# S5 scan states: from a transpose on VectorE and TensorE to a ScalarE copy and two DMAs through DRAM

## The chip, the cores and the metric

The kernel runs on one core of one Trainium2 chip. Times are device microseconds of one execution, from the core's own clock. The kernel before took 1846.21 us, the median of 3 runs (1843.55 to 1846.67).

A core has five engines, each with a queue of its own that it works through strictly in order: TensorE (PE: matmuls; its weight loads are shown as PEld), VectorE (DVE), ScalarE (ACT), GpSimd (POOL) and SyncE (SP, which here only issues DMAs). DMAs can be issued from the queues of SP, ACT and POOL. The profile shows 16 DMA engines behind them.

## What is computed

A trunk of two layers on 256 frames of width 2048, in float32: a gated linear attention layer, then an S5 layer (a complex-diagonal state-space model), each with adaLN modulation and a post-LayerNorm residual. Everything that matters here is in the S5 mixer:

```
proj = u_in @ w_in
u, z = jnp.split(proj, 2, axis=-1)
...
_, _, x_r, x_i = lax.associative_scan(_linear_recurrence_combine, (a_r, a_i, bu_r, bu_i), axis=1)
return jnp.einsum('blgp,gip->blgi', x_r, cr_b) - jnp.einsum('blgp,gip->blgi', x_i, ci_b)
...
y = jax.nn.gelu(y)
y = y * jax.nn.sigmoid(y @ w_glu + b_glu)
y = y * jax.nn.silu(z)
return y @ w_out
```

The 4096 channels are 256 groups of 16; each group has 64 complex states.

## The kernel before

**Chunks.** The recurrence isn't run frame by frame. The 256 frames are 32 chunks of 8. For every chunk the kernel computes the sum of the inputs that reach the chunk's end, runs the recurrence over the 32 chunk states (`scan`, L1180), and then forms the outputs of a chunk as two matmul products: the eight inputs of the chunk by an in-chunk kernel (`mt`), and the state at the chunk's start by powers of the transition times C (`wc`). The groups are worked in 32 blocks, numbered f, of eight groups each. The states of all blocks lie in one buffer, `sx`, with the state index on the partitions and chunk, real/imaginary and group in the free dimension; its first half holds f 0 to 15, its second half f 16 to 31.

**The projections.** `st_step` (L171) does a step of a projection: 24 matmuls of 128x256. Each weight tile is split into a rounded part (`hi`, a cast on ScalarE, L145) and a remainder (`lo`, a subtraction on VectorE, L146), because one product is made of three. There are four buffers for weight tiles and three each for the two parts, so a cast waits until TensorE has finished the step three before. The u projection (`su`) runs first, with the inputs of the chunks beside it; then the z projection (`sz`), 64 steps in eight groups (loop at L1270).

**The output side** runs beside `sz`. A list `bg` holds small pieces of work; after each projection step `pump` (L96) takes `Y_RATE` pieces from it on average. For each f the list has, in this order: three scan steps of the second half (while there are any), `cside(f)`, `xstage(f - 1)`, `ystage(f - 2)`: 126 pieces over 56 steps.

- `cside(f)` (L1263) loads the next block of C rows and powers (`cload`, three DMAs into `cl`, since the third third of the columns is the first one with the real and imaginary halves of the partitions swapped), loads the in-chunk kernel `mt` (`mload`, 512 KB), and multiplies `cl` to the two weights `wc` on VectorE (L1074, L1075).
- `xstage(f)` (L1236) makes the chunk states an operand of TensorE: a 32x32-block transpose on VectorE from `sx` to `xT`, two 128x128 transposes on TensorE into PSUM (`psxs`), and a copy on ScalarE to `xS`.
- `ystage(f)` (L1247) does 48 small matmuls (`psy`), a transpose on VectorE (`yt`) and a GELU on ScalarE into `U`.

The C rows, B rows and powers come from `rec` in DRAM. They are written there from GpSimd's queue much earlier, during the first layer (`prep_b`, `prep_c`, `prep_pow`).

**What sets the order.** The program is written in the order of these calls, and the order on each engine is then made by a scheduler, which moves an instruction ahead when it expects its operands to be ready. So an instruction of `bg` may stand several projection steps away from where the list puts it. Semaphore waits follow from the buffers: an instruction that writes a tile waits until the last reader of that buffer is done, and a DMA counts as a reader until it has landed.

Of the kernel before, what the change touches and what calls it, by code (L numbers as in the profile page):

```python
# [8 lines left out]
F32 = mybir.dt.float32  # L9
# [6 lines left out]
P = 128  # L16
D = 2048
E = 4096
T = 256
# [14 lines left out]
def trunk(ctx, tc, x, c, ln_g, ln_b, ada_w, ada_b, gla_w_in, gla_gate_w2, gla_gate_b, gla_norm_g,  # L34
# [45 lines left out]
    def psx(name):  # L80
        return ax.tile([P, 512], F32, tag="ax", name=name)
# [10 lines left out]
    bg = []  # L92
# [506 lines left out]
    def prep_pow(t):  # L599

        pw = SM["pw"]
        pd = s8t(f"pd{t}", [8, 2, 2, 64])
        for h in range(2):
            S.copy(pd[:, :, :, h, :], pw[:, :, :, t * 64:t * 64 + 64])
        lc = s8t(f"lc{t}", [16, 2, 8, 8])
        for ri in range(2):
            for nb in range(2):
                ps = psx(f"pspw{t}{ri}{nb}")
                for i in range(4):
                    n = nb * 4 + i  # L610
# [3 lines left out]
        wdma(rec[:, 16 * t:16 * t + 16, 128:256], lc.rearrange("p f r g n -> p f (r g n)"))  # L614

    def to_rows(src, i_of, t, o, nm):
        got = {}

        def step(ib):
            if ib == 0:  # L620
                got["a"] = s8t("rows" + nm, [128, 16])
            a = got["a"]
            ps = psx(f"psr{nm}{ib}")
            for i in range(4):
                PE.transpose(ps[:, i * P:(i + 1) * P], i_of(src(), 4 * ib + i), ident)
            S.copy(a[:, :, 4 * ib:4 * ib + 4].rearrange("p g i -> p i g"), ps.rearrange("p (i g) -> p i g", i=4))
            if ib == 3:
                av = a.rearrange("p (f g) i -> p f (g i)", f=16)
                wdma(rec[:, 16 * t:16 * t + 16, o:o + 128], av)

        return [lambda ib=ib: step(ib) for ib in range(4)]

    def prep_b(t):
        got = {}

        def load():
            bi = s8t(f"bin{t}", [2, 64, 16])
            got["bi"] = bi
# [17 lines left out]
        return [load], [comp] + to_rows(lambda: got["b"], lambda s, i: s[:, :, i], t, 256, f"b{t}")  # L656

    def prep_c(t):
        got = {}

        def load():
            ci = s8t(f"cin{t}", [2, 16, 64])
            got["ci"] = ci
            dma(ci[:, 0], s5_c_re[0, t * P:(t + 1) * P])
            dma(ci[:, 1], s5_c_im[0, t * P:(t + 1) * P])

        def comp():
            ci = got["ci"]
# [5 lines left out]
        return [load], [comp] + to_rows(lambda: got["c"], lambda s, i: s[:, i].rearrange("g r p -> g (r p)"), t, 0, f"c{t}")  # L674
# [376 lines left out]
    def bload(f2):  # L1051

        a = tp.tile([P, 2, 384], F32, tag="rb", name=f"rb{f2}", bufs=2)
        dma(a[:, :, 0:256], rec[:, 2 * f2:2 * f2 + 2, 128:384])
        for h in range(2):
            dma(a[64 * h:64 * h + 64, :, 256:384], rec[64 - 64 * h:128 - 64 * h, 2 * f2:2 * f2 + 2, 256:384])
        rb[f2] = a

    rc = {}
# [1 line left out]
    def kload(f2):  # L1061

        a = rc[f2] = tp.tile([P, 2, 144], F32, tag="rc", name=f"rc{f2}", bufs=2)
        dma(a, rec[:, 2 * f2:2 * f2 + 2, 0:144])

    wb = {}

# [144 lines left out]

    def cload(f):
        a = tp.tile([P, 384], F32, tag="cl", name=f"cl{f}", bufs=2)
        dma(a[:, 0:256], rec[:, f, 0:256])
        for h in range(2):
            dma(a[64 * h:64 * h + 64, 256:384], rec[64 - 64 * h:128 - 64 * h, f, 0:128])
        cl[f] = a

    def cunit(f):  # L1220
        a = cl[f]
        w = [tp.tile([P, 8, 8, 16], F32, tag=f"wc{i}", name=f"wc{i}{f}", bufs=2) for i in range(2)]
        powmul(w[0], w[1], a[:, 0:128], a[:, 256:384], a[:, 128:256])
        wc[f] = w

    kap = dk[:, :]
# [6 lines left out]

    xss = {}

    def xstage(f):  # L1236
        xt_ = tp.tile([P, 2, 4, 32], F32, tag="xt", name=f"xT{f}", bufs=1)
        n = 2 * (f % 16)
        V.transpose(xt_, sx[:, f // 16, 0:32, :, n:n + 2].rearrange("p c r b -> p b r c"))
        px = psx(f"psxs{f}")  # L1240
        for b in range(2):
            PE.transpose(px[:, b * P:(b + 1) * P], xt_[:, b].rearrange("p r l -> p (r l)"), ident)
        xs = tp.tile([P, 2, 128], F32, tag="xs", name=f"xS{f}", bufs=2)
        S.copy(xs, px[:, :T].rearrange("p (b r) -> p b r", b=2))
        xss[f] = xs

    def ystage(f):  # L1247
        xs = xss[f]
        py = psx(f"psy{f}")
        U = Uv(f)  # L1250
        for b in range(2):
            o = py[:, b * P:(b + 1) * P]
            for q in range(4):
                PE.matmul(o[32 * q:32 * q + 32], lhsT=U[:, 2 * q + b], rhs=mt[f][:, :, 2 * q + b, :], start=True, stop=False)
# [6 lines left out]
        S.activation(U, yt, AF.Gelu_apprx_tanh)  # L1261

    def cside(f):  # L1263
        if f < 31:
# [5 lines left out]
    for g in range(8):  # L1270
        banks = [psm(f"sz{g}{f}") for f in range(4)]
        for kp in range(8):
            w = split(wload(sw, 2 * kp, E + g * 512, f"sz{g}{kp}"), f"sz{g}{kp}")
            st_step(banks, u1, w, kp, 15)
            if g == 0:
                bstep(1 + kp % 2)
            pump(SCAN_RATE if g == 0 else Y_RATE)
        for f in range(4):
            i = (g * 4 + f) % 8
            if g % 2 == 0 and f == 0:  # L1280
                zs.append(s8t(f"zs{g // 2}", [8, T]))
# [172 lines left out]
```

## Time and profile before

| | us |
|---|---|
| median of 3 runs | 1846.21 |
| the profiled execution | 1847.81 |
| its span, first to last instruction | 1846.0 |
| ScalarE busy over the span | 895.7 |
| GpSimd busy over the span | 85.6 |
| one state transpose on VectorE (median of 32) | 0.633 |
| one `wc` product on VectorE (median of 32) | 1.218 |
| `mt`, issue to landing (median of 32) | 7.7 |

The profile is of one execution. "Busy" counts an engine's instructions, but matmuls are pipelined and their durations overlap, so the cost of a matmul is read from the distance between two starts. A row of the timeline gives start, duration, engine, line, operation, output and inputs; in brackets is how long the engine stood idle before it, and what released it. The DMA share of a window is the mean busy share of the 16 DMA engines.

### The profile page before, as it was taken

The page shows a single profiled execution, that of the slowest core. Times are in us where ns is not written, and L with a number is a line of the kernel's source. Part 1 is how long each engine was busy: PE and PEld are TensorE (multiplying, and loading weights), DVE is VectorE, ACT ScalarE, POOL GpSimd, SP SyncE. Part 2 cuts the span into 40 slices and gives each one's busy share as a digit, 9 for nine tenths or more (in the row PEclk, how much of TensorE's full clock was granted, in tenths as well). Part 3 has the DMA queues.
Part 4 walks back from the last instruction along what each step waited for, and adds up shares of the span by engine and source line. Part 5 has one row for each costly group of instructions (what it writes and reads, how often), then busy time and mean ns, then how long its engine had stood idle before and what let it go on. Part 6 is the DMA issues. An engine that isn't in the chain of part 4 may idle for free.

```text
span 1846.0 us, 33780 instructions
## 1 busy us (share of the span) xinstructions
PE 1795.7 (97%) x13555; PEld 1587.8 (86%) x13555; DVE 1401.8 (76%) x1862; ACT 895.7 (49%) x1266; POOL 85.6 (5%) x94
## 2 busy tenths in 40 slices
PE   7999999999999999999999999999999999999997
PEld 5776897899999888799998989989888888888885
DVE  4877667879989988686799779888677775557556
ACT  4432557555556333554454444545544544444332
POOL 0000000000000000002232300000000000000000
PEclk9999999999999999999999999999999999999998
DMA  9996885889889998577666567899788886668653
GB/s 342 380 325 226 293 263 165 262 270 322 290 277 324 331 356 287 171 248 212 197 175 196 173 194 219 232 254 240 220 276 267 270 277 209 190 192 325 193 183 92
DMA packets 246101, 457.86 MB, mean 248 GB/s; under 512 B 19828, under 2 KB 49198, under 8 KB 244662
## 3 DMA queue, kind: packets, MB, share of 16 engines
q1 hardware_dynamic: 239320, 436.02, 73.8%
q0 software_dynamic: 5856, 18.63, 3.1%
q8 instruction: 106, 1.74, 0.4%
q10 hardware_dynamic: 768, 1.05, 0.2%
q14 instruction: 51, 0.42, 0.1%
HBM read 437.01 MB, written 18.61 MB: 247 GB/s over the span
## 4 chain that ended last, share of the span: by engine, by line
PE 83%; DVE 9%; DMA 3%; issue 2%; ACT 2%; POOL 0%; SPq 0%; DVEq 0%; ACTq 0%; POOLq 0%
PE gl L192 13%; PE gl L193 7%; PE op L168 6%; PE op L167 6%; PE op L169 6%; PE z L182 3%; PE z L180 3%; PE z L181 3%; PE v L168 3%; PE v L169 3%; PE v L167 3%; PE su L180 2%; PE su L181 2%; PE su L182 2%; PE sz L180 2%
## 5 line engine op out<-in xcount | busy, mean ns | idle before, releaser
L146 DVE TENSOR_TENSOR logl<-wgl,higl 128x1024 fp32r<-128x1024 f32 x128 | 156.6, 1223 | 115.7 <-ACT higl L145 109.2
L145 ACT CAST higl<-wgl 128x1024 fp32r<-128x1024 f32 x128 | 134.4, 1050 | 170.7 <-PE gl L192 163.0
L192 PE MATMUL gl<-yp,higl 128*128 128x512 f32 x512 | 179.3, 395 | 0.1
L192 PE MATMUL gl<-yb,higl 128*128 128x512 f32 x512 | 179.1, 395 | 0.0
L145 ACT CAST hio<-wo 128x1024 fp32r<-128x1024 f32 x95 | 100.2, 1055 | 154.7 <-PE op L169 134.4
L146 DVE TENSOR_TENSOR loo<-wo,hio 128x1024 fp32r<-128x1024 f32 x95 | 116.1, 1223 | 67.1 <-ACT hio L145 66.6
L315 DVE SCALAR_TENSOR_TENSOR acc<-wa,cs,acc 128x512 f32<-128x512 f32 x217 | 162.1, 747 | 4.0 <-DMA wa<-in_ada_w 1.1
L180 PE MATMUL sz<-u1h,hisz 128*128 128x256 f32 x512 | 151.0, 295 | 1.3 <-ACT zs L1282 1.2
L180 PE MATMUL su<-u1h,hisu 128*128 128x256 f32 x512 | 151.8, 298 | 0.0
L180 PE MATMUL z<-u0h,hiz 128*128 128x256 f32 x512 | 148.7, 290 | 0.0
L182 PE MATMUL sz<-u1h,losz 128*128 128x256 f32 x512 | 145.6, 285 | 3.1 <-DVE losz L146 3.1
L182 PE MATMUL su<-u1h,losu 128*128 128x256 f32 x512 | 146.7, 287 | 0.0
L181 PE MATMUL su<-u1l,hisu 128*128 128x256 f32 x512 | 146.4, 286 | 0.0
L182 PE MATMUL z<-u0h,loz 128*128 128x256 f32 x512 | 144.9, 283 | 0.6 <-DVE loz L146 0.6
L181 PE MATMUL sz<-u1l,hisz 128*128 128x256 f32 x512 | 145.4, 284 | 0.0
L181 PE MATMUL z<-u0l,hiz 128*128 128x256 f32 x512 | 144.7, 283 | 0.0
L193 PE MATMUL gl<-yb,logl 128*128 128x256 f32 x512 | 142.9, 279 | 0.0
L193 PE MATMUL gl<-yp,logl 128*128 128x256 f32 x512 | 142.2, 279 | 0.0
L145 ACT CAST hisz<-wsz 128x1024 fp32r<-128x1024 f32 x64 | 67.0, 1050 | 117.7 <-PE sz L181 62.0
L192 PEld LDWEIGHTS gl<-yp,higl 128*128 128x128 f32 x512 | 95.9, 188 | 22.8 <-issue 0.7
L192 PEld LDWEIGHTS gl<-yb,higl 128*128 128x128 f32 x512 | 96.0, 188 | 22.6
L168 PE MATMUL v<-lov,u0h 128*128 128x512 f32 x256 | 103.6, 406 | 6.9 <-DVE lov L146 6.8
(321 smaller groups left out, 4974.0 us busy)
## 6 DMA issues: line engine op xcount, KB each, us to landing
wgl<-in_s_w_glu SPq DMA_DIRECT2D x128, 512.0 KB, 4.5
wa<-in_ada_w SPq DMA_DIRECT2D x116, 512.0 KB, 5.3
wv<-in_gla_w_in SPq DMA_DIRECT2D x64, 512.0 KB, 5.8
wz<-in_gla_w_in SPq DMA_DIRECT2D x64, 512.0 KB, 5.1
wsu<-in_s_w_in SPq DMA_DIRECT2D x64, 512.0 KB, 4.3
wsz<-in_s_w_in SPq DMA_DIRECT2D x64, 512.0 KB, 5.7
wo<-in_s_w_out SPq DMA_DIRECT2D x64, 512.0 KB, 4.6
a<-in_ada_w SPq DMA_DIRECT2D x31, 1024.0 KB, 10.8
```

What stands on the lines that cost most here:

```text
L145: S.copy(hi, w)
L146: last_lo[0] = V.tensor_tensor(lo, w, hi.bitcast(F32), op=ALU.subtract).ins
L167: PE.matmul(banks[tt], lhsT=uh, rhs=hi[:, kk, :], start=(k == first), stop=False)
L168: PE.matmul(banks[tt], lhsT=uh, rhs=lo[:, kk, :], start=False, stop=False)
L169: last_mm[0] = PE.matmul(banks[tt], lhsT=ul, rhs=hi[:, kk, :], start=False, stop=(k == last)).ins
L180: PE.matmul(o, lhsT=wh, rhs=u.hi(k), start=(k == first), stop=False)
L181: PE.matmul(o, lhsT=wh, rhs=u.lo(k), start=False, stop=False)
L182: last_mm[0] = PE.matmul(o, lhsT=wl, rhs=u.hi(k), start=False, stop=(k == last)).ins
L192: PE.matmul(banks[f], lhsT=hi[:, kk, fs], rhs=u.both(k), start=(k == 0), stop=False)
L193: PE.matmul(banks[f][:, :T], lhsT=lo[:, kk, fs], rhs=u.hi(k), start=False, stop=(k == last))
L315: V.scalar_tensor_tensor(acc[0], w[:, kk, :], cs[:, k:k + 1], acc[0], op0=ALU.mult, op1=ALU.add)
```

## The change

The state of block f no longer goes through a VectorE transpose and two TensorE transposes. ScalarE copies it from `sx` to `xT` in another order of the free dimension (`xwrite`) and writes it to a DRAM tile `dx[f]` with a DMA from its own queue (128 KB, 1 KB for each partition). A DMA from GpSimd's queue (`xread`) reads it back with the partition index made of chunk and real/imaginary, in runs of 256 bytes, into `xS`. `xT` has one buffer, as before; `xS` has three instead of two, `yt` one instead of two.

Since the partitions of `xS` now come in another order (chunk before real/imaginary), the weights `wc` must have that order too: `cload` permutes the rows as it reads `rec`, and the swapped third is stored in `rec` (which grows from 384 to 512 columns), so that `cload` is one DMA instead of three. That takes two more GpSimd writes after each of the two C row tiles. The other edits in `rec` move columns only. The list `bg` has 158 pieces now, with `xwrite` one block ahead of `xread`, and `Y_RATE` is 2.9.

```diff
-    rec = dp.tile([P, 32, 384], F32, name="rec")
+    rec = dp.tile([P, 32, 512], F32, name="rec")
+    dx = dp.tile([32, P, 256], F32, name="dx")
...
                 wdma(rec[:, 16 * t:16 * t + 16, o:o + 128], av)
+                if o == 128:
+                    for h in range(2):
+                        wdma(rec[64 * h:64 * h + 64, 16 * t:16 * t + 16, 0:128], av[64 - 64 * h:128 - 64 * h])
...
-    Y_RATE = 2.311
+    Y_RATE = 2.9
...
     def cload(f):
         a = tp.tile([P, 384], F32, tag="cl", name=f"cl{f}", bufs=2)
-        dma(a[:, 0:256], rec[:, f, 0:256])
-        for h in range(2):
-            dma(a[64 * h:64 * h + 64, 256:384], rec[64 - 64 * h:128 - 64 * h, f, 0:128])
+        dma(a, rec[:, f, 0:384].rearrange("(r l) x -> l r x", r=4))
...
-    def xstage(f):
-        xt_ = tp.tile([P, 2, 4, 32], F32, tag="xt", name=f"xT{f}", bufs=1)
+    def xwrite(f):
+        xt_ = tp.tile([P, 4, 2, 32], F32, tag="xt", name=f"xT{f}", bufs=1)
         n = 2 * (f % 16)
-        V.transpose(xt_, sx[:, f // 16, 0:32, :, n:n + 2].rearrange("p c r b -> p b r c"))
-        px = psx(f"psxs{f}")
-        for b in range(2):
-            PE.transpose(px[:, b * P:(b + 1) * P], xt_[:, b].rearrange("p r l -> p (r l)"), ident)
-        xs = tp.tile([P, 2, 128], F32, tag="xs", name=f"xS{f}", bufs=2)
-        S.copy(xs, px[:, :T].rearrange("p (b r) -> p b r", b=2))
-        xss[f] = xs
+        S.copy(xt_, sx[:, f // 16, 0:32, :, n:n + 2].rearrange("p c r b -> p r b c"))
+        S.dma_start(dx[f], xt_.rearrange("p r b c -> p (r b c)"))
+
+    def xread(f):
+        xs = xss[f] = tp.tile([P, 4, 2, 32], F32, tag="xs", name=f"xS{f}", bufs=3)
+        wdma(xs.rearrange("p q b c -> p q (b c)"), dx[f].rearrange("(q l) (r x) -> (l r) q x", q=4, r=4))
...
-                    PE.matmul(o[32 * q:32 * q + 32], lhsT=xs[:, b, 32 * q:32 * q + 32],
+                    PE.matmul(o[32 * q:32 * q + 32], lhsT=xs[:, q, b],
...
-        yt = tp.tile([P, 8, 32], F32, tag="yt", name=f"yt{f}", bufs=2)
+        yt = tp.tile([P, 8, 32], F32, tag="yt", name=f"yt{f}", bufs=1)
...
-                if 1 <= f < 33:
-                    bg.append(lambda f=f: xstage(f - 1))
+                for i in range(0 if f == 0 else f + 1, min(f + 2, 32)):
+                    bg.append(lambda i=i: xwrite(i))
+                if f < 32:
+                    bg.append(lambda f=f: xread(f))
```

Three places show what the scheduler makes of it. In the names, the number behind `hisz`, `wsz` and `sz` is the group of the z projection and the step in it, the number behind `xT`, `xS`, `psxs` and `psy` is f.

ScalarE's queue in the middle of the stage, around the step 4, 6. Before:

```order
L145 CAST hisz45_12955<-wsz45_12953 128x1024
L1261 ACTIVATE U1_7510<-yt8_12760 128x8x32
L1244 COPY xS10_12808<-psxs10_12805 128x256
L145 CAST hisz46_13030<-wsz46_13028 128x1024
L1261 ACTIVATE U1_7510<-yt9_12835 128x8x32
L1244 COPY xS11_12883<-psxs11_12880 128x256
```

After:

```order
L145 CAST hisz45_12947<-wsz45_12945 128x1024
L1241 COPY xT19_13336<-sx_7511 128x256
L1242 DMA dx_200<-xT19_13336 128x256
L1241 COPY xT20_13407<-sx_7511 128x256
L1242 DMA dx_200<-xT20_13407 128x256
L145 CAST hisz46_12988<-wsz46_12986 128x1024
L1262 ACTIVATE U1_7515<-yt9_12800 128x8x32
L1241 COPY xT21_13478<-sx_7511 128x256
L1242 DMA dx_200<-xT21_13478 128x256
```

The copies of the states no longer keep pace with f: they stand well ahead of the GELU of their own block, up to two of them between two casts. In the whole queue the copies xT0 to xT15 stand behind the 12th to the 25th cast of the z projection and xT16 to xT31 behind the 35th to the 46th, the second half after the last scan step.

TensorE's queue, at the end of a projection step that is followed by psy. Before:

```order
L182 MATMUL sz53_13148<-u1h0_7385,losz52_13295 128x256
L1242 MATMUL psxs16_13324<-ident_89,xT16_13322 128x128 x2
L1254 MATMUL psy15_13329<-mt15_13127,U1_7510 32x128 x4
L1257 MATMUL psy15_13329<-wc015_13129,xS15_13222 32x128 x4
L1257 MATMUL psy15_13329<-wc115_13130,xS15_13222 32x128 x4
```

After:

```order
L181 MATMUL sz53_13125<-u1l0_7392,hisz52_13240 128x256
L182 MATMUL sz53_13125<-u1h0_7390,losz52_13241 128x256
L1255 MATMUL psy15_13270<-mt15_13048,U1_7515 32x128 x4
L1258 MATMUL psy15_13270<-wc015_13050,xS15_13087 32x128 x4
L1258 MATMUL psy15_13270<-wc115_13051,xS15_13087 32x128 x4
```

The two transposes are gone; psy follows the projection directly and stands behind the same projection step as before.

SP's queue where the output side begins. Before:

```order
L136 DMA wsz16_11666<-in_s5_w_in 128x2x512
L1215 DMA cl0_11398<-rec_197 128x256
L1217 DMA cl0_11398<-rec_197 64x128 x2
L1215 DMA cl1_11478<-rec_197 128x256
L1217 DMA cl1_11478<-rec_197 64x128 x2
L1231 DMA mt0_11482<-dk_198 128x1x1024
L1231 DMA mt1_11564<-dk_198 128x1x1024
```

After:

```order
L136 DMA wsz16_11665<-in_s5_w_in 128x2x512
L1219 DMA cl0_11403<-rec_197 128x1x384
L1219 DMA cl1_11481<-rec_197 128x1x384
L1233 DMA mt0_11483<-dk_198 128x1x1024
L1233 DMA mt1_11571<-dk_198 128x1x1024
L136 DMA wsz17_11729<-in_s5_w_in 128x2x512
```

Each cl is one DMA, and the next weight tile stands two blocks of cl earlier than before.

More of the change, by code (lines that the diff above doesn't have):

```diff
@@ L613, in prep_pow @@
                 S.activation(lc[:, :, ri, :, nb * 4:nb * 4 + 4].rearrange("p f g n -> p n f g"), pv, AF.Identity, scale=sgn if ri else 1.0)
-        wdma(rec[:, 16 * t:16 * t + 16, 128:256], lc.rearrange("p f r g n -> p f (r g n)"))
+        wdma(rec[:, 16 * t:16 * t + 16, 256:384], lc.rearrange("p f r g n -> p f (r g n)"))
     def to_rows(src, i_of, t, o, nm):
@@ L654, in comp @@
             got["b"] = bb.rearrange("g r p i -> g (r p) i")
-        return [load], [comp] + to_rows(lambda: got["b"], lambda s, i: s[:, :, i], t, 256, f"b{t}")
+        return [load], [comp] + to_rows(lambda: got["b"], lambda s, i: s[:, :, i], t, 384, f"b{t}")
     def prep_c(t):
@@ L672, in comp @@
             got["c"] = cc
-        return [load], [comp] + to_rows(lambda: got["c"], lambda s, i: s[:, i].rearrange("g r p -> g (r p)"), t, 0, f"c{t}")
+        return [load], [comp] + to_rows(lambda: got["c"], lambda s, i: s[:, i].rearrange("g r p -> g (r p)"), t, 128, f"c{t}")
     (lb0, cb0), (lc0, cc0), (lb1, cb1), (lc1, cc1) = prep_b(0), prep_c(0), prep_b(1), prep_c(1)
@@ L1053, in bload @@
         a = tp.tile([P, 2, 384], F32, tag="rb", name=f"rb{f2}", bufs=2)
-        dma(a[:, :, 0:256], rec[:, 2 * f2:2 * f2 + 2, 128:384])
+        dma(a[:, :, 0:256], rec[:, 2 * f2:2 * f2 + 2, 256:512])
         for h in range(2):
-            dma(a[64 * h:64 * h + 64, :, 256:384], rec[64 - 64 * h:128 - 64 * h, 2 * f2:2 * f2 + 2, 256:384])
+            dma(a[64 * h:64 * h + 64, :, 256:384], rec[64 - 64 * h:128 - 64 * h, 2 * f2:2 * f2 + 2, 384:512])
         rb[f2] = a
@@ L1063, in kload @@
         a = rc[f2] = tp.tile([P, 2, 144], F32, tag="rc", name=f"rc{f2}", bufs=2)
-        dma(a, rec[:, 2 * f2:2 * f2 + 2, 0:144])
+        dma(a, rec[:, 2 * f2:2 * f2 + 2, 128:272])
     wb = {}
@@ L1222, in cunit @@
         w = [tp.tile([P, 8, 8, 16], F32, tag=f"wc{i}", name=f"wc{i}{f}", bufs=2) for i in range(2)]
-        powmul(w[0], w[1], a[:, 0:128], a[:, 256:384], a[:, 128:256])
+        powmul(w[0], w[1], a[:, 128:256], a[:, 0:128], a[:, 256:384])
         wc[f] = w
@@ L1256, in ystage @@
                 for q in range(4):
-                    PE.matmul(o[32 * q:32 * q + 32], lhsT=xs[:, b, 32 * q:32 * q + 32],
+                    PE.matmul(o[32 * q:32 * q + 32], lhsT=xs[:, q, b],
                               rhs=w[:, 2 * q + b].rearrange("p n i -> p (n i)"), start=False, stop=(w is wc[f][-1]))
-        yt = tp.tile([P, 8, 32], F32, tag="yt", name=f"yt{f}", bufs=2)
+        yt = tp.tile([P, 8, 32], F32, tag="yt", name=f"yt{f}", bufs=1)
         V.transpose(yt, py[:, :T].rearrange("p (b t i) -> p t b i", b=2, t=8))
-        S.activation(U, yt, AF.Gelu_apprx_tanh)
+        S.activation(U, yt.rearrange("p t c -> p (t c)").rearrange("p (b r) -> p b r", b=2), AF.Gelu_apprx_tanh)
     def cside(f):
```

## The prediction

> **What bounds the kernel now.** I read the page's busy times first, then a table of windows over the stage that the change touches, then the instructions behind single tiles, and last the order of the new program.
>
> ```profile
> PE 1795.7 (97%) x13555; PEld 1587.8 (86%) x13555; DVE 1401.8 (76%) x1862; ACT 895.7 (49%) x1266; POOL 85.6 (5%) x94
> ```
>
> TensorE is busy nearly throughout, so only what shortens TensorE's stream, or what makes it wait, can move the end. The table of windows cuts the z projection of the S5 layer from 1085 us on, where the output side of the scan runs in the background.
>
> ```profile
> 1085.00:1164.00 79.00, 78.70 (x926) 75.33 (x925) 76.31 (x139) 36.02 (x53) 0.00 (x0) 0.99 0.79 229
> 1164.00:1212.00 48.00, 48.00 (x714) 44.98 (x714) 43.37 (x49) 24.53 (x38) 0.00 (x0) 1.00 0.90 242
> 1212.00:1254.00 42.00, 40.11 (x563) 37.61 (x565) 33.42 (x39) 21.28 (x32) 0.00 (x0) 0.96 0.99 247
> 1254.00:1294.00 40.00, 40.00 (x608) 37.18 (x602) 37.78 (x46) 24.61 (x43) 0.00 (x0) 1.00 0.98 246
> ```
>
> The columns are PE, PEld, DVE, ACT and POOL busy, then clock, DMA share and GB/s. To 1164 VectorE (76.31 of 79) and TensorE are both full, because the scans of the second half run there; afterwards TensorE is full, and the DMA engines go from 0.90 to 0.99 busy. ScalarE is about half busy everywhere. So three resources stand close together here, and a change that relieves two of them meets the third.
>
> **What goes.** The tile view of the transposed states, the same tile's instructions alone in the first window (PE, PEld, DVE), and the longest wait of TensorE at the stage's start:
>
> ```profile
> L1242 PE MATMUL psxs<-ident,xT x64: 270/272/328, 1079.9 to 1288.5; 128*128 128x128 f32 x64
> L1239 DVE STREAM_TRANSPOSE xT<-sx x32: 572/633/665, 1073.9 to 1284.5; 128x256 f32<-128x256 f32 x32
> L1244 ACT COPY xS<-psxs x32: 351/354/394, 1080.9 to 1289.9; 128x256 f32<-128x256 f32 x32
> ...
> 1085.00:1164.00 79.00, 3.37 (x18) 2.20 (x18) 5.78 (x9) 0.99 0.79 229
> PE sz L182 <- DVE losz L146: 3.1, 1, 3.1
> ```
>
> Matmuls overlap, so 272 ns isn't the price of one. That is read from starts, once with the transposes in between and once where psy follows the projection directly:
>
> ```profile
> 1093.46 0.28 PE L182 MATMUL sz<-u1h,losz 128*128 128x256 f32 x1
> 1093.67 0.43 PE L1254 MATMUL psy<-mt,U 128*32 128x128 f32 x8
> ...
> 1163.98 0.42 PE L1254 MATMUL psy<-mt,U 128*32 128x128 f32 x8
> ...
> 1165.43 0.38 PE L180 MATMUL sz<-u1h,hisz 128*128 128x256 f32 x1
> ...
> 1168.27 0.28 PE L182 MATMUL sz<-u1h,losz 128*128 128x256 f32 x1
> 1168.39 0.38 PE L1242 MATMUL psxs<-ident,xT 128*128 128x128 f32 x2
> 1168.70 0.42 PE L1254 MATMUL psy<-mt,U 128*32 128x128 f32 x8
> ```
>
> From the last projection matmul to psy it is 0.43 us with them and 0.21 without: 0.22 us for each f. Some 24 of the 32 f lie after 1164, so TensorE can give 24 x 0.22 = 5.3 us there. Before 1164 VectorE loses nine transposes, 5.8 us; but TensorE is late next. Of the 926 matmuls in that window 18 are transposes and 8 x 48 belong to psy; 524 remain, 22 projection steps. A step is 2.96 us (1165.43 to 1168.39); psy takes 1.45 (1163.98 to 1165.43). That makes 22 x 2.96 + 8 x 1.45 = 76.7 of 79, so about 2.3 us come out, not 5.8. The 3.1 us wait near 1081 is TensorE waiting for a VectorE subtraction queued behind products that wait for cl; cl now comes in one DMA instead of three. I count 1 us of it, between 0 and 3.1. **Gains: 5.3 + 2.3 + 1 = 8.6 us, if nothing is given back.**
>
> The faster pace number (2.9 for 2.311) only serves more list entries: 158/2.9 and 126/2.311 are both 54.5 of 56 steps. SP loses 64 DMA issues; what that is worth at the stage's start is in the 1 us.
>
> **What is added on ScalarE, and the wait.** Each f has a copy out of the scan buffer and a DMA issue, in place of the copy out of PSUM.
>
> ```profile
> L626 ACT COPY rowsc<-psrc x8: 1055/1068/1086, 274.3 to 351.6; 128x512 f32<-128x512 f32 x8
> ...
> L1410 ACTq DMA_DIRECT2D out<-big x16: 321/432/452, 1829.2 to 1842.1; - x16
> ```
>
> No row shows a copy that reads with this stride. It lies between 0.354 us (L1244, same size) and 0.53 (half of the strided rowsc copy); I take 0.45. The issue is 0.43. Work on ScalarE thus grows by 0.53 us per f, 17 us over a stage in which it idles 100; alone it would hide. But xT has one buffer, so copy f+1 can't start before write f has landed, and the copies stand among the casts hisz of the weights, which TensorE needs. The order shown above has f 0 to 15 behind the 12th to the 25th cast and f 16 to 31 behind the 35th to the 46th. In the profile of before those casts start here:
>
> ```profile
> 1071.29 1.05 ACT L145 CAST hisz<-wsz 128x1024 fp32r<-128x1024 f32 x1 [1.12 <-PE sz L181]
> ...
> 1119.19 1.05 ACT L145 CAST hisz<-wsz 128x1024 fp32r<-128x1024 f32 x1 [1.36 <-PE sz L181]
> ...
> 1157.81 1.08 ACT L145 CAST hisz<-wsz 128x1024 fp32r<-128x1024 f32 x1
> ...
> 1202.55 1.05 ACT L145 CAST hisz<-wsz 128x1024 fp32r<-128x1024 f32 x1 [3.46 <-PE sz L181]
> ```
>
> So 15 turns of copy, issue and landing must fit into 47.9 us, and 15 more into 44.7. What a landing takes, issue included:
>
> ```profile
> cl<-rec SPq DMA_DIRECT2D x32, 128.0 KB, 3.3
> dk<-ks POOLq DMA_DIRECT2D x32, 64.0 KB, 3.1
> out<-big ACTq DMA_DIRECT2D x16, 64.0 KB, 2.3
> ...
> DMA to landing us min/median/max: 2.1/3.1/4.8
> ```
>
> The bounds are 2.3 us (ScalarE's own writes at the quiet end of the kernel) and 4.8 (the slowest dk write, the last row). The nearest rows are the dk writes to DRAM, half as large in a less loaded stage, 3.1, and cl, the same 128 KB in this stage, 3.3. I take 3.2. A turn is 0.45 + 3.2 = 3.65 us, and 15 are 54.8. Casts run about two steps ahead of TensorE: some 6 us, less the cast (1.05) and about as much for the subtraction after it, a cushion of about 4. Early 54.8 - 47.9 - 4 = 2.9 us are lost, late 54.8 - 44.7 - 4 = 6.1. Behind the waiting copy stand the next cast, and behind that VectorE's subtraction and TensorE's step; the activation U waits too, and with it yt, which now has one buffer.
>
> These 9.0 us replace the gains inside the two stretches. What is left of the 8.6 is the piece from 1119 to 1158 (about 1.0), and from 1203 on 16 x 0.22 = 3.5, of which the DMA part below takes the larger share; I keep 1. **Sum: 9.0 - 2.0 = 7 us longer.**
>
> The Trainium skill's page "DMA: Bandwidth & Descriptors", section "Anatomy of one DMA", fits a DMA as 2.0 us fixed, mostly the write receipt, plus the bytes at 436 GB/s. Worked out from it, an estimate for 128 KB is 2.3 us, and 15 turns of 2.75 are 41 us, so nothing would be lost; the rows at 3.1 and 3.3, from loaded stages, stand against it.
>
> **What is added on the DMA engines.**
>
> ```profile
> q1 hardware_dynamic: 239320, 436.02, 73.8%
> q0 software_dynamic: 5856, 18.63, 3.1%
> ...
> PE psy L1254 <- DMA mt<-dk: 1.9, 1, 1.9
> ```
>
> Shares are of 16 engines over 1846 us: both queues take 49 to 50 engine-us per MB. A write and a read of 0.131 MB take 2 x 0.131 x 50 / 16 = 0.82 us of all engines per f; at the rate between 1212 and 1254 (0.99 x 16 / 0.247 = 64 per MB) 1.05. The read's runs of 256 bytes occur in no row, so it may be dearer. cl moves the same bytes in longer runs, 0 to 0.2 us saved. I take 0.8 net, 32 x 0.8 = 26 us. From 1085 to 1294 the engines were busy 0.79 x 79 + 0.90 x 48 + 0.99 x 42 + 0.98 x 40 = 186 of 209 us; 212 doesn't fit into 209, nor into 209 less the gains. Where ScalarE's wait already stretches the stage, the transfers fit into the longer time; where it doesn't, they are the bound.
>
> The skill's same page, section "Issuing engines are not separate DMA queues", says that DMAs issued by ScalarE, SyncE and GpSimd run on the same 16 engines, so that other queues save only the issue. No run here shows it yet; had the new queues engines of their own, this term would be zero.
>
> **Hidden edits.** GpSimd, which did nothing in these windows, issues the 32 reads, and three xS buffers give each two f of lead. The extra rec writes (2 MB, 2 x 50 / 16 = 6 us of engine time, about 300 to 355 us) lie under the v projection, and rec is read hundreds of us later; uncovered they would cost 1 to 2 us.
>
> **The rivals.**
> - **Short landings, faster.** Writes land in 2.3 to 2.8 us, as at the quiet end. A turn is then at most 3.25, 15 are 48.8, and the cushion hides the rest. The gains hold less 0 to 2 for DMA: 1837 to 1840, say 1838.5. It decides from a landing of about 2.9 us. For it: the 2.3 row; against: DMA at 0.79 to 0.99.
> - **The DMA engines bind.** Landings are near 2.9, ScalarE is late nowhere, but mt and wsz queue among the new transfers. 212 us at full share against 209 is +3; with packets squeezed closer, -1: 1845 to 1850, say 1848. For it: mt already stops TensorE once; against: TensorE waited for a DMA there only this once, 1.9 us.
>
> **How the numbers follow.** The profiled execution took 1847.8 us (span 1846.0), 1.6 above the median 1846.2; I carry differences to the median. Forecast (ScalarE waits for its own writes): 0.48, 1846.2 + 7 = 1853. Short landings: 0.29. DMA engines bind: 0.23, half of it within 0.2% (3.7 us, about what a measurement tells from no change), where a small part of the forecast lies too. Faster 0.30, same 0.16, slower 0.54. The range runs from the short-landing time to a landing of 3.8 us (a turn of 4.25, 63.8 for 15: 11.9 + 15.1 - 2 = 25 longer): 1837 to 1871.
>
> **What would show it.** Right: casts hisz idle behind copies xT that wait on a DMA, landings of dx at 3 us or more, TensorE idle between 1073 and 1210 but hardly from 1215 on, VectorE's busy time 20 us smaller. Wrong: dx landing under 2.9 us with casts still waiting for TensorE, or psy waiting for mt or xS in the last third, which would make it the DMA engines. If copies xT take 0.7 us or more, the turn is longer for another reason than the landing.

## The result and the profile after

The changed kernel takes **1893.2 us** (median of 4 runs, 1891.2 to 1897.8) against 1845.9 for the kernel before on the same chip: a ratio of **1.0254, 95% interval 1.0238 to 1.0269**, 47 us longer. The forecast was 1853, its range 1837 to 1871. The sign was right, and ScalarE does wait behind its own writes; the loss was nearly seven times the 7 us of the forecast.

The page of the changed kernel, its busy times and its DMA queues (packets, MB, share of 16 engines):

```profile
PE 1802.0 (95%) x13491; PEld 1592.5 (84%) x13491; DVE 1385.6 (73%) x1830; ACT 902.0 (48%) x1262; POOL 113.8 (6%) x130
...
q1 hardware_dynamic: 234200, 436.02, 71.3%
q0 software_dynamic: 7968, 24.93, 4.3%
q10 hardware_dynamic: 5376, 5.25, 1.0%
```

VectorE is 16 us less busy (20 were forecast), and TensorE has 64 instructions fewer, yet its busy time is 6 us longer. Where the time went is bounded by the tile view of psy, which has the first and the last start of the output matmuls. First the kernel before, then the changed one:

```profile
L1254 PE MATMUL psy<-mt,U x512: 270/273/421, 1093.7 to 1294.1; 128*32 128x128 f32 x171
```

```profile
L1255 PE MATMUL psy<-mt,U x512: 270/273/423, 1094.0 to 1337.1; 128*32 128x128 f32 x171
```

From first to last it was 200.4 us and is 243.1: 42.7 of the 43.4 us by which the spans differ (1846.0 and 1889.4) lie here. I call this length **the output stretch** below. The table of windows cuts it (columns as before: PE, PEld, DVE, ACT, POOL busy, then clock, DMA share, GB/s), first for the kernel before:

```profile
sum 200.00, PE 197.81 PEld 186.23 DVE 182.44 ACT 103.72 POOL 0.00; mean PE 98.90 PEld 93.11 DVE 91.22 ACT 51.86 POOL 0.00
```

```profile
1094.00:1160.00 66.00, 52.93 (x587) 49.84 (x587) 48.04 (x88) 30.25 (x42) 4.49 (x6) 0.84 0.70 200
1160.00:1200.00 40.00, 39.26 (x536) 37.23 (x535) 28.83 (x42) 15.86 (x22) 4.48 (x6) 1.00 0.89 251
1200.00:1260.00 60.00, 47.14 (x580) 43.53 (x579) 35.69 (x36) 26.15 (x38) 5.23 (x7) 0.86 0.73 207
1260.00:1337.00 77.00, 66.31 (x969) 61.74 (x971) 62.23 (x71) 37.82 (x57) 7.48 (x10) 0.98 0.97 255
sum 243.00, PE 205.64 PEld 192.34 DVE 174.79 ACT 110.07 POOL 21.68; mean PE 51.41 PEld 48.09 DVE 43.70 ACT 27.52 POOL 5.42
```

TensorE was idle 2.2 us of the stretch (200 - 197.81) and is idle 37.4 now (243 - 205.64). It is also busy 7.8 us longer for fewer matmuls; its granted clock is 0.84 and 0.86 in two of the four windows. The idle time lies in three of them: the two in which ScalarE writes, and the last, where ScalarE writes no more and the DMA share is 0.97. Who waited for whom, TensorE and then ScalarE (us in total, times, longest):

```profile
PE sz L180 <- ACT zs L1283: 18.3, 5, 6.9
PE psy L1255 <- DMA mt<-dk: 9.4, 5, 3.8
PE sz L180 <- ACT hisz L145: 8.6, 3, 4.0
PE sz L182 <- DVE losz L146: 5.0, 5, 3.1
```

```profile
ACT xT L1241 <- DMA dx<-xT: 71.7, 23, 6.9
```

ScalarE stands still for 71.7 us behind its own writes, 23 times, 3.1 us each. TensorE sees this as 18.3 us behind zs (the activation that empties the PSUM banks of a finished group of columns), 8.6 behind the casts and 5.0 behind VectorE. The timeline of ScalarE shows one such piece:

```profile
1177.45 0.33 ACTq L1242 DMA_DIRECT2D dx<-xT  x1
...
1183.29 0.66 ACT L1241 COPY xT<-sx 128x256 f32<-128x256 f32 x1 [1.55 <-DMA dx<-xT]
1183.98 0.33 ACTq L1242 DMA_DIRECT2D dx<-xT  x1
1184.35 1.05 ACT L145 CAST hisz<-wsz 128x1024 fp32r<-128x1024 f32 x1 [0.40 <-PE sz L182]
1185.31 0.41 ACT L1262 ACTIVATE U<-yt 128x256 f32<-128x256 f32 x1
1188.67 0.66 ACT L1241 COPY xT<-sx 128x256 f32<-128x256 f32 x1 [2.95 <-DMA dx<-xT]
1189.35 0.33 ACTq L1242 DMA_DIRECT2D dx<-xT  x1
1189.72 1.05 ACT L145 CAST hisz<-wsz 128x1024 fp32r<-128x1024 f32 x1 [0.40 <-ACT xT L1241]
1196.73 0.67 ACT L1241 COPY xT<-sx 128x256 f32<-128x256 f32 x1 [5.96 <-DMA dx<-xT]
1197.43 0.33 ACTq L1242 DMA_DIRECT2D dx<-xT  x1
1202.07 0.62 ACT L1241 COPY xT<-sx 128x256 f32<-128x256 f32 x1 [4.67 <-DMA dx<-xT]
```

Between two copies there is at most one cast, with or without a U, and then nothing: copy to copy takes 5.3 to 8.1 us here, where TensorE needs a cast every 2.96. And this is what TensorE does meanwhile:

```profile
1200.83 0.28 PE L181 MATMUL sz<-u1l,hisz 128*128 128x256 f32 x1
1200.95 0.28 PE L182 MATMUL sz<-u1h,losz 128*128 128x256 f32 x1
1204.26 0.58 PE L180 MATMUL sz<-u1h,hisz 128*128 128x256 f32 x1 [3.03 <-ACT hisz L145]
...
1208.25 0.41 PE L182 MATMUL sz<-u1h,losz 128*128 128x256 f32 x1
1208.46 0.41 PE L180 MATMUL sz<-u1h,hisz 128*128 128x256 f32 x1
```

It waits 3.03 us, and then starts a matmul every 0.21 us where it was 0.12 before, so part of a wait is paid again in slower matmuls. The table of windows has the granted clock of that piece at half:

```profile
1204.06:1210.89 6.83, 6.17 (x32) 5.63 (x36) 6.23 (x7) 2.95 (x6) 0.00 (x0) 0.50 0.56 174
```

### The profile page after: what moved, and what is told of

It reads as the page before. It is cut to its first block, busy times and chain, and to the rows that moved or that the text cites. A ratio compares the mean times of both kernels' runs of the same rounds, so it can differ in the third digit from the quotient of the medians.

```text
span 1889.4 us, 33624 instructions
## 1 busy us (share of the span) xinstructions
PE 1802.0 (95%) x13491; PEld 1592.5 (84%) x13491; DVE 1385.6 (73%) x1830; ACT 902.0 (48%) x1262; POOL 113.8 (6%) x130
## 3 DMA queue, kind: packets, MB, share of 16 engines
q8 instruction: 106, 1.74, 0.4%
## 4 chain that ended last, share of the span: by engine, by line
PE 77%; DMA 9%; DVE 6%; ACT 4%; issue 3%; POOL 1%; ACTq 0%; DVEq 0%; SPq 0%; POOLq 0%
PE gl L192 13%; PE gl L193 6%; PE op L168 6%; PE op L169 6%; PE op L167 6%; DMA dx<-xT 5%; PE z L182 3%; PE z L180 3%; PE z L181 3%; PE v L168 3%; PE v L169 3%; PE v L167 2%; PE su L180 2%; PE su L181 2%; PE su L182 2%
## 5 line engine op out<-in xcount | busy, mean ns | idle before, releaser
L180 PE MATMUL sz<-u1h,hisz 128*128 128x256 f32 x512 | 155.5, 304 | 26.8 <-ACT zs L1283 18.3
L182 PE MATMUL sz<-u1h,losz 128*128 128x256 f32 x512 | 150.5, 295 | 5.0 <-DVE losz L146 5.0
L181 PE MATMUL sz<-u1l,hisz 128*128 128x256 f32 x512 | 149.7, 293 | 0.0
L180 PEld LDWEIGHTS sz<-u1h,hisz 128*128 128x128 f32 x512 | 103.6, 202 | 35.0 <-ACT zs L1283 19.3
L146 DVE TENSOR_TENSOR losz<-wsz,hisz 128x1024 fp32r<-128x1024 f32 x64 | 77.6, 1220 | 69.9 <-ACT hisz L145 65.5
## 6 DMA issues: line engine op xcount, KB each, us to landing
a<-in_ada_w SPq DMA_DIRECT2D x31, 1024.0 KB, 10.7
```

The source lines that it names most:

```text
L146: last_lo[0] = V.tensor_tensor(lo, w, hi.bitcast(F32), op=ALU.subtract).ins
L180: PE.matmul(o, lhsT=wh, rhs=u.hi(k), start=(k == first), stop=False)
L181: PE.matmul(o, lhsT=wh, rhs=u.lo(k), start=False, stop=False)
L182: last_mm[0] = PE.matmul(o, lhsT=wl, rhs=u.hi(k), start=False, stop=(k == last)).ins
```

## The experiments

Two theories stood after this. **Own wait**: ScalarE sits behind its landing write in the midst of the casts. **DMA engines**: the added transfers fill the 16 engines, and mt and the rest come late. All runs beside the kernel before on the same chip. The stretch and all waits are from the profile, which is of one execution; its time stands in the third column. In e2, e5 and e8 it is 6 to 11 us away from the median, so there the stretch doesn't speak for the median to the microsecond.

| run | median us | profiled run us | ratio to before (95%) | output stretch us |
|---|---|---|---|---|
| before | 1846 | 1847.8 | 1 | 200.4 |
| changed | 1893.2 | 1891.2 | 1.0254 (1.0238-1.0269) | 243.1 |
| e2_no_dma | 1842.1 | 1851.2 | 0.9979 (0.9967-0.9992) | 198.7 |
| e3_load | 1919.9 | 1916.0 | 1.0393 (1.0372-1.0414) | 204.0 |
| e5_xt2 | 1876.6 | 1887.9 | 1.0172 (1.0135-1.0209) | 238.2 |
| e6_ring | 1861.7 | 1860.6 | 1.0082 (1.0063-1.0102) | 211.9 |
| e3b_load | 1870.2 | 1870.4 | 1.0140 (1.0099-1.0181) | 212.8 |
| e4_no_read | 1884.2 | 1882.4 | 1.0209 (1.0182-1.0235) | 234.9 |
| e8_small_write | 1882.5 | 1876.4 | 1.0194 (1.0167-1.0221) | 229.1 |
| e7_pool | 1896.2 | 1899.3 | 1.0268 (1.0240-1.0297) | 251.6 |
| e9_cl | 1848.7 | 1845.3 | 1.0019 (1.0005-1.0034) | 199.3 |
| e10_ring5 | 1864.1 | 1864.2 | 1.0108 (1.0087-1.0129) | 216.1 |
| e12_ring_twice | 1880.9 | 1881.0 | 1.0193 (1.0166-1.0220) | 232.1 |
| e13_no_transpose | 1838.4 | 1838.5 | 0.9965 (0.9949-0.9980) | 194.9 |

**No dx at all (e2_no_dma).** From the changed kernel:

```diff
-        S.copy(xt_, sx[:, f // 16, 0:32, :, n:n + 2]...)
-        S.dma_start(dx[f], xt_...)
-        wdma(xs..., dx[f]...)
+        S.copy(xs, sx[:, f // 16, 0:32, :, n:n + 2]...)
```

> The changed kernel without the write and the read of dx: ScalarE copies the scan states straight into xS, so the transposition over partitions is left out. What stays is the copy of 0.65 us, the loss of TensorE's and VectorE's transposes, and cl in one DMA. If the 47 us come from the write's landing (ScalarE waits for its own DMA) or from the DMA engines, all of it goes and the gains of the prediction show: 1836 to 1843 us. If the dearer copy on ScalarE, or another of the kept edits, makes the loss, the time stays above 1860.

The loss goes: 4 us below the kernel before. The dearer copy (0.67 us here) and ScalarE's work as such cost nothing that shows. But the 8.6 us of gains that the prediction counted are not there in full; e9 and e13 take them apart.

**The traffic alone, first try (e3_load).** From the kernel before:

```diff
         S.copy(xs, px[:, :T]...)
+        S.dma_start(dx[f], xs...)
+        for i in range(2):
+            xz = tp.tile([P, 2, 64], ..., bufs=1)
+            wdma(xz, dv[:, 2 * i:2 * i + 2])
```

> The kernel before with the same traffic added and nobody waiting for it: after each copy xS, ScalarE writes xS to dx (128 KB), and GpSimd reads it back, in two halves, into a tile that nobody uses. xS has three buffers and yt one, as in the changed kernel. If ScalarE's wait for its own write is the loss, the traffic alone costs little: 1846 to 1853 us. If the DMA engines are the bound, it costs most of the 47 us here too: 1875 or more.

A miss of the experiment's design. The 64 half reads share one buffer and go one after the other; at the stage's end VectorE's first instruction in the room that comes free waits for the last of them:

```profile
DVE ones L1314 <- DMA xz<-dx: 70.4, 1, 70.4
```

These 70 us are nearly the whole loss of 74, and are no cost of the traffic. The output stretch, 204.0 us, is hardly longer than before, but the reads run on far beyond it, so the run decides nothing.

**Two buffers for xT (e5_xt2).**

```diff
-        xt_ = tp.tile(..., tag="xt", bufs=1)
+        xt_ = tp.tile(..., tag="xt", bufs=2)
-        xs = ... tp.tile(..., tag="xs", bufs=3)
+        xs = ... tp.tile(..., tag="xs", bufs=2)
```

> The changed kernel with two xT buffers (and two xS for three, for the room): a copy waits for the write before the last. If the wait for the own write is the loss, a turn is shared by two copies, some 2.5 us instead of 4.6, less than a step of the projection (2.96): 1842 to 1858 us. If the DMA engines bind, the same transfers still have to pass: 1875 or more.

Neither number came: by the medians about a third of the loss goes. The profile is of the slowest of the four executions, 11 us above the median, and its stretch is only 4.9 us shorter than the changed kernel's, so it shows the kind of the waits better than their size. ScalarE's wait for dx halves, to 36.5 us in 16 waits. With the second buffer the copies move closer together instead of getting out of the way (the last one starts at 1213.8 us, in the changed kernel at 1249.5), so casts still stand behind landing writes; and TensorE's wait for mt doubles, to 20.3 us.

**One ring for xT and xS (e6_ring).**

```diff
-        xt_ = tp.tile(..., tag="xt", bufs=1)
+        xt_ = tp.tile(..., tag="xs", bufs=3)
```

> The changed kernel, all its transfers kept, but xT and xS take turns in one ring of three buffers. Copy f+2 (or f+3) then takes a buffer that the output matmuls psy have just given back, so that the copies stand in ScalarE's order where TensorE uses the states, spread over the whole stage, no longer one behind each cast. If the loss is that ScalarE sits behind its own landing write in the midst of the casts, most of it goes although no transfer is saved: 1840 to 1856 us. If the DMA engines bind: 1875 or more.

With every transfer kept and one buffer fewer, two thirds of the loss go: 1893.2 - 1861.7 = 31.5 us. That is outside both expected ranges. The waits of TensorE and of ScalarE's copies in this run:

```profile
PE psy L1258 <- DMA xS<-dx: 9.2, 8, 2.5
PE psy L1255 <- DMA mt<-dk: 5.7, 4, 3.0
PE sz L182 <- DVE losz L146: 3.9, 1, 3.9
PE sz L180 <- ACT zs L1283: 0.8, 1, 0.8
```

```profile
ACT xT L1241 <- PE psy L1258: 19.9, 24, 4.0
...
ACT xT L1241 <- DMA dx<-xT: 7.4, 2, 6.6
```

The waits for the casts are gone from TensorE's list, and that for zs is down from 18.3 us to 0.8. The landings have not become shorter (by the semaphore updates in the traces 6.8 us at the mean, against 3.8 in the changed kernel, and GpSimd's reads wait 102.2 us for the writes), but hardly a cast stands behind them now. What is left are above all waits for transfers, after 1160 us, at a DMA share of 1.01 in this run:

```profile
1160.00:1300.00 140.00, 125.09 (x1773) 115.16 (x1776) 103.37 (x107) 70.25 (x104) 16.44 (x22) 0.96 1.01 272
```

So both theories hold, for two parts of the time. The ring changes two things at once, the place of the copies and whom they wait for; e5 (a second buffer, the copies still crowded) suggests that the place is the larger part, but no run has it alone.

**The traffic alone, second try (e3b_load).** As e3, with one read for each f and two xS buffers.

> Again the kernel before with the traffic added and nobody waiting for it, now with each read in one DMA (the two halves of e3 went one after the other and outlived the stage): after each copy xS, ScalarE writes xS to dx, GpSimd reads it back into a tile that nobody uses. xS keeps its two buffers, yt has one. If the wait for the own write is the whole loss: 1846 to 1852 us. If the traffic makes what e6 left over (some 16 us): 1856 to 1866. If it makes all: 1880 or more.

1870, between the ranges, but 10 us of it are again the last reads after the stage (VectorE waits 10.1 us for xz). The output stretch is free of that: 212.8 against 200.4, 12.4 us, and ScalarE waits for dx only once in it, 7.2 us for the 71.7 of the changed kernel. e6 against e2, from the other side, gives 211.9 - 198.7 = 13.2. By the medians e6 is 19.6 us over e2; the other 6 us lie outside the stretch, where single profiles differ by up to 10 us (the first psy starts at 1089.2 us in e13's and at 1098.9 in e2's). So the transfers cost 13 to 20 us.

**The wait without the traffic (e4_no_read, e8_small_write).** From the changed kernel; the second line is e8 alone:

```diff
-        wdma(xs..., dx[f]...)
+        nc.gpsimd.memset(xs, 0.0)
-        S.dma_start(dx[f], xt_...)
+        S.dma_start(dx[f][:, 0:32], xt_...[:, 0:32])
```

> The changed kernel without the read of dx: GpSimd fills xS with zeros, so the states' part of the output is left out. The writes and ScalarE's wait for them stay as they are. If the wait is two thirds of the loss and the landing is long because of the other transfers, the landings shrink somewhat with half of the added traffic gone: 1862 to 1882 us, and the copies xT still wait for their writes. If the traffic is the loss, half of the 47 us goes, without waits of the copies: about 1868. The waits of the copies tell them apart, not the time.

> As e4 (no read, zeros in xS), and the write carries 32 of the 256 columns, 16 KB for 128 KB, in as many rows: the rest of the states isn't written. The wait for the own write stays. If a landing is made of its fixed part and of what stands ahead of it on the 16 engines, its own bytes matter little and the time is within 8 us of e4. If its bytes make it, the waits of the copies nearly go: 15 us or more below e4.

Without the reads 9 us come back, to 2 us above the first range, and the waits of the copies stay; with writes of an eighth of the bytes as well, about 2 more. ScalarE's wait for its writes, e4 and then e8:

```profile
ACT xT L1241 <- DMA dx<-xT: 67.3, 23, 5.7
```

```profile
ACT xT L1241 <- DMA dx<-xT: 61.2, 21, 7.1
```

That is 2.9 us for each wait, with 128 KB and with 16 KB. What a landing is made of can be counted in the traces, which hold the 16 semaphore updates of each of these writes; the last one is the landing. In e8 the writes land in 1.4 to 7.0 us, 3.5 at the mean. The six during whose first microsecond no packet of another queue moved took 1.41 to 1.45. So the fixed part and the rows make 1.4 us together, and the rest comes up only where other transfers are under way; the write's own bytes hardly matter. With hardly any traffic of dx left, e8 is still 40 us slower than e2 (30 by the two stretches): **the wait alone makes most of the loss.** (30 to 40 from the wait and 13 to 20 from the traffic are together more than the 42.7 or 47 of the changed kernel. A likely reason is that the transfers have more time where ScalarE stretches the stage; no run tests it.)

**Copy and write on GpSimd (e7_pool).**

```diff
-        S.copy(xt_, sx[...])
-        S.dma_start(dx[f], xt_...)
+        nc.gpsimd.tensor_copy(xt_, sx[...])
+        wdma(dx[f], xt_...)
```

> The changed kernel with the copy, the write and the read all on GpSimd; ScalarE has no part in them. The transfers stay. If ScalarE's wait is two thirds of the loss and GpSimd keeps up (copy, landing and two issues within some 6 us for each f): 1852 to 1866 us. If GpSimd's turn is longer than that, it becomes the bound, TensorE waits for xS, and the time is above 1880; in that case the run says little on ScalarE.

The second case. GpSimd's copy takes 0.70 us at the median, and it waits for its own landing write 30 times, 101.5 us in all; now the states come late: TensorE waits 35.1 us for xS. A chain of copy, landing, copy with one buffer is slow on either engine. GpSimd's queue has the reads too, though, which wait 61.2 us for psy to give buffers back, so the run says little on ScalarE.

**The cl part alone (e9_cl).** The kernel before with rec's layout and the single DMA of the changed one, without the permuted rows:

```diff
-        dma(a[:, 0:256], rec[:, f, 0:256])
-        for h in range(2):
-            dma(a[64 * h:64 * h + 64, 256:384], rec[64 - 64 * h:128 - 64 * h, f, 0:128])
+        dma(a, rec[:, f, 0:384])
```

> The kernel before with only the cl part of the change: rec gets the swapped half as a piece of its own, and cl comes in one DMA for three. The transposes and the copy out of PSUM stay, nothing goes through dx. The prediction gave this part 1 us of the stall at the stage's start and 0 to 0.2 us of DMA time for each f: 1841 to 1847 us. If the longer rec (more bytes written and a wider row) cost something, it shows here as more than 1850.

No gain, and between the two expectations: 0.19% longer (0.05 to 0.34%), some 3.5 us. The stall at the stage's start stays at 3.2 us, and TensorE loses time where the rows are written. The window from 300 to 400 us, the kernel before, then this run:

```profile
300.00:400.00 100.00, 97.84 (x572) 83.37 (x572) 82.51 (x103) 60.52 (x81) 2.31 (x2) 1.00 0.77 250
```

```profile
300.00:400.00 100.00, 94.17 (x544) 79.73 (x543) 80.29 (x99) 55.60 (x75) 3.97 (x4) 0.98 0.80 258
```

3.7 us more idle time (97.84 - 94.17); the changed kernel has 94.20 there. The traces say where: two of the four extra writes into rec, of 512 KB each, are issued near 352 us, and the four take 9.6 us to land at the median. Some 10 us after these two a cast waits 8.1 us for its weight tile, where it waited 4.0 before, and TensorE waits 2.6 us for copies that stand behind this cast. No run moves these writes alone.

**Five buffers in the ring, and a second read (e10_ring5, e12_ring_twice).** Both from e6:

```diff
-        xt_ = tp.tile(..., tag="xs", bufs=3)
+        xt_ = tp.tile(..., tag="xs", bufs=5)
-        xs = ... tp.tile(..., tag="xs", bufs=3)
+        xs = ... tp.tile(..., tag="xs", bufs=5)
```

```diff
         wdma(xs..., dv)
+        xz = tp.tile([P, 4, 64], ..., bufs=1)
+        wdma(xz, dv)
```

> As e6, with five buffers in the ring for three (a constant, dT, moves out of the permanent tiles and gives its room back before this stage). A copy then takes its buffer four f ahead of psy, for two to three in e6. In e6 TensorE waited 9 us for xS. If what e6 left (16 us over the kernel before) was that lateness, most of it goes: 1845 to 1853 us. If it is that the DMA engines are full from about 1160 us on, little of it goes, and TensorE waits for mt in place of xS: 1855 to 1864.

> As e6, and GpSimd reads each dx a second time, into a tile that nobody uses. One read takes 0.75 us of all 16 engines (the queue of these reads takes 24 us more in the changed kernel than before, for 32 of them). If the DMA engines are what e6 waits for, in the part with some 24 of the 32 f, that is 18 us more: 1872 to 1888. If they have room and only lateness counts: 1861 to 1868.

Five buffers don't help (1864.1, at the upper end of the second range). The waits for xS go, and TensorE waits for mt in their place, 17.1 us for e6's 5.7:

```profile
PE psy L1257 <- DMA mt<-dk: 17.1, 10, 4.1
PE sz L184 <- DVE losz L148: 3.1, 1, 3.1
PE sz L182 <- ACT zs L1285: 2.7, 1, 2.7
```

The second read costs 19 us (1880.9 - 1861.7). Its queue takes 5.2% of 1879.2 us against 4.3% of 1858.7, 17.8 us of all 16 engines, 0.56 for each f. (The 0.75 of the expectation was too high: it had counted the additional rec writes, which go through the same queue.) A transfer that nobody uses is paid nearly one for one, as it would be if the engines are the bound in this part. It isn't proof: xz has one buffer, so GpSimd's queue waits 108.2 us for the second reads to land (20 waits), the next xS reads stand behind them, and TensorE's wait for xS grows from 9.2 to 13.1 us as well. The larger growth is that for mt, which doesn't pass through GpSimd's queue: from 5.7 to 15.1.

**Without the transposes (e13_no_transpose).** From the kernel before:

```diff
-        V.transpose(xt_, sx[...])
-        for b in range(2):
-            PE.transpose(px[:, b * P:(b + 1) * P], ..., ident)
-        S.copy(xs, px[:, :T]...)
+        S.copy(xs..., sx[...])
```

> The kernel before without the transposes alone: ScalarE copies the scan states straight into xS (the transposition over partitions is left out), cl, rec and everything else as before. The prediction took 5.3 us from TensorE and 2.3 us from VectorE, together 7.6: 1836 to 1840 us. If mt, already late in the run without dx (7.4 us of TensorE's waits), takes part of it back because a faster stage asks for the same transfers sooner: 1840 to 1844.

0.35% shorter (0.20 to 0.51%): 6.5 us, for the prediction's 7.6. The other case is not excluded by the interval, but mt is late by only 2.3 us in this profile.

## Why the prediction was right in kind and wrong in size

By differences of the medians the 47 us are: -4 for all edits without dx (e2), +19.6 for dx's transfers with the copies out of the way (e6 less e2), +31.5 for the copies in the midst of the casts (changed kernel less e6). By the output stretches they are -1.7, +13.2 and +31.2, together 42.7. The forecast named the largest part, and put it at 9.0 us.

1. **TensorE's 5.3 and VectorE's 2.3 us: their sum was right.** e13 measured 6.5 (3.7 to 9.4) for the forecast 7.6; it doesn't tell the two apart.
2. **The start stall and cl, 1 us gained: wrong sign, small.** The stall stays, and the longer rec, "hidden", costs 3.7 us of TensorE near 300 us where at most 2 had been granted. The gains, 8.6 in the forecast, measured about 4 (e2).
3. **The copy, 0.45 us: mis-sized.** It takes 0.655, above its upper bound of 0.53: the rows had no copy with this stride, and the bound was half of a copy with another one.
4. **The turn of copy, issue and landing, 3.65 us: mis-sized, and this is the step that failed.** It was set at 3.65 us, with a landing of 3.2, and at most 4.25. The first 16 writes are issued from 1074.80 to 1140.58 us and the other 16 from 1177.45 to 1250.1:

```profile
1140.58 0.33 ACTq L1242 DMA_DIRECT2D dx<-xT  x1
```

```profile
L1242 ACTq DMA_DIRECT2D dx<-xT x32: 326/326/374, 1074.8 to 1250.1; - x32
```

   That makes turns of 65.8 / 15 = 4.4 and 72.7 / 15 = 4.8 us. In the prediction's own sum these give 65.8 - 47.9 - 4 = 13.9 and 72.7 - 44.7 - 4 = 24.0; less the 2 us of gains it is 36 us longer, near 1882 and outside the range, against e6's 31.5 for this mechanism. (The turns include some waiting for TensorE, so this is a check and no proof.) By the semaphore updates the landings were 3.5 us at the mean in the first stretch and 3.9 in the second. So of the 29 us that are new in this sum, the landings make 15, the copy 6, and 8 are other work and waits between two copies. The 11 us from 1882 to 1893 are left to point 7. A landing isn't one number: the chain of waits has 4.62 to 7.35 us for neighbours of one another,

```profile
1177.45 5.82 DMA dx<-xT
...
1183.98 4.66 DMA dx<-xT
...
1189.35 7.35 DMA dx<-xT
...
1197.43 4.62 DMA dx<-xT
```

   and e8 shows that other transfers make it, not the bytes. In the changed kernel, too, the seven writes during whose first microsecond no packet of another queue moved landed in 1.70 to 1.74 us, the other 25 in 1.71 to 7.4, 4.4 at the mean. I had taken medians of writes from quieter stages and of reads; in a serial chain the mean under load counts, long landings and all.
5. **"The next cast, then VectorE, then TensorE": incomplete.** The largest of TensorE's waits, 18.3 of 41 us, is for zs, which stands in ScalarE's queue at the end of a group of columns. The cushion of 4 us was worked out for casts alone; zs has hardly any, since a group takes four of the five banks, and the next one soon needs those that zs empties. Two of its five waits, 6.5 and 6.9 us, are directly behind copies that waited for dx.
6. **A long wait costs more than its length.** The clock wasn't in the sum at all. After a wait TensorE's matmuls start 0.21 us apart and not 0.12, and its clock is 0.84 and 0.86 over two windows of 126 us together. The Trainium skill's page "TensorE: Matmul & The Clock Gate", section "What's actually happening", says that the array falls to half its clock after an idle window of some 3.4 us and needs as long a busy one to come back; the trace agrees on the half (0.50 from 1204.06 to 1210.89 us), but there a wait of 3.03 us was enough.
7. **The DMA engines, "212 of 209": right size, wrong division.** The added engine time was set at 26 us. By the queues it is 77.1% of 1846.0 before (73.8, 3.1 and 0.2) and 78.0% of 1858.7 in e6 (72.7, 4.3 and 1.0): 26.5 us, from rounded shares. (In e9, with the longer rec and the one cl but no dx, the sum is 77.2% of 1843.5, the same 1423 us as before, so the 26.5 are dx's.) But it was set against the free time of the whole stretch, and the free time lies before 1164 us, while 24 of the 32 f lie after it. By the prediction's own rows the engines were busy 0.90 x 48 + 0.99 x 42 + 0.98 x 40 = 124 of 130 us there; 24 x 0.82 = 20 more make 144, which is 14 too many, not 3. e6 and e3b measured 13 and 12 in the stretch, and e12 nearly one for one. That the transfers fit into the time that ScalarE's wait adds was true of a part at most: the late reads and mt came after the last write, at a DMA share of 0.97, and TensorE stood idle 10.7 us there.

What should show it: casts idle behind copies xT that wait for a DMA did show, and so did landings over 3 us (3.8 at the mean of the 32), and VectorE is less busy, though by 16 us and not 20. "TensorE idle hardly from 1215 on" didn't, since the late writes went on to 1250 us and the engines filled after that; psy waiting for mt in the last third was named as the sign of the rival, and came too. The two were taken as alternatives, and both are true at once. The rival "short landings" fell: it had 2.3 to 2.8 us for all of them, and 20 of the 32 took 2.9 us or more.

e2 and e13 are faster than the kernel before, but they leave the transposition over partitions out; none of the others is. e13 bounds what the transposes are worth, 6.5 us, and the way through DRAM costs twice that in the transfers alone, with hardly a wait of ScalarE for its writes left (e6).

## What to carry to other kernels

- A DMA that an in-order compute engine issues from a single buffer makes that engine wait for the landing; ask what stands behind the next use of the buffer, and take the mean landing in the stage's own traffic, with its long ones, not a median from a quieter one.
- Free DMA time counts only where the new transfers have to pass. Cut the sum at the points where the demand changes, and add up two resources that are near their limits, instead of taking them as rivals.
- If TensorE's matmuls get slower after a wait, add that to the wait.

## What the runs showed that I had not expected

- Eight times fewer bytes left a landing as long as it was: 2.9 us for each wait with 16 KB as with 128 KB (e8, e4), with the DMA engines 0.76 busy over the stage (e8). Where nothing else moved, 112 KB more cost 0.3 us (1.41 to 1.45 us and 1.70 to 1.74).
- The page's list of DMA issues and the waits disagree for the same writes: the list has a median of 2.1 us from issue to landing, yet the chain has pieces of 4.6 to 7.4 us. The list has a landing for only five of these 32 writes, since the records of the semaphores are incomplete for the others. From the 16 updates behind each issue the median is 3.6 us, the mean 3.8 and the longest 7.4.

```profile
dx<-xT ACTq DMA_DIRECT2D x32, 128.0 KB, 2.1
xS<-dx POOLq DMA_DIRECT2D x32, 128.0 KB, 5.9
```

- A transfer from another queue still shares the bound. The Trainium skill's page "DMA: Bandwidth & Descriptors", section "Issuing engines are not separate DMA queues", says that all of them share 16 engines; e12 agrees, where reads from GpSimd's queue that nobody used delayed mt from SyncE's (15.1 us of waits for 5.7):

```profile
PE psy L1258 <- DMA mt<-dk: 15.1, 7, 4.0
```
